# Block sums for the seven-product matmuls: taken one step later, and queued behind the last convolution on VectorE

## The chip, the cores and the metric

The kernel runs on one core of a Trainium2 chip. Its time is the device time of one execution in microseconds (us). Three executions of the kernel before took 2258.66, 2259.78 and 2261.68 us; the median is 2259.78 us. The engines are TensorE (PE; its weight loads are the rows PEld), VectorE (DVE), ScalarE (ACT), GpSimd (POOL) and SyncE (SP). SP and POOL also issue the DMAs that matter here.

## The reference

One inference step of a two-layer streaming encoder, on 1024 prompt frames and 64 sample frames (1088 columns), with 1024 channels. Layer 0 mixes by windowed attention, layer 1 by a diagonal state-space model. Each layer ends in a gated feed-forward net with a causal convolution of width 3; the change touches only this part:

```python
def conv_ffn(h, prev, w_up, conv_w, conv_b, w_down):
    t = h.shape[1]
    up = h @ w_up
    full = jnp.concatenate([prev.astype(up.dtype), up], axis=1)
    c = conv_b
    for j in range(CONV_WIDTH):
        c = c + conv_w[j] * full[:, j:j + t]
    y = (jax.nn.gelu(c[..., :D_FF]) * c[..., D_FF:]) @ w_down
    return y, full[:, -(CONV_WIDTH - 1):]
```

`w_up` is 1024 by 5632, `w_down` 2816 by 1024, `D_FF` is 2816. Everything is float32.

## The kernel before

**Layout.** Channels lie on the 128 partitions, frames along the free axis, in three blocks of 384, 384 and 320 columns. A float32 product is made of three matmuls of rounded parts: each operand is split into a high part (a copy on ACT) and a low part (a subtraction on DVE), and `mm3` (L220) issues L223, L224 and L225. A weight tile is loaded by SP (`raw`), split into `whl` (L193 on ACT and L194 on DVE, or L216 for both), and then used. `unit` (L165) starts the load of a weight tile two tiles ahead of the one that is used.

**The up-projection.** `ffn` runs over 22 gates f. A gate makes two tiles of 128 channels (f and 22 + f): the matmuls give `u`, `conv` (L415) makes `t` from it in one instruction on ACT (L419) and two on DVE (L420, L421; the second is kept as `last_conv`), and the first `t` goes through GELU, is multiplied by the second (L437), and is stored to the DRAM tensor `gd` (L438, L439). In layer 0, and in layer 1 for f under 5, a tile is 3 blocks of 8 by 3 matmuls, evicted by DVE (L411, L413). In layer 1 from f = 5 on, the first two blocks of both tiles are made by `seven` (L491): seven products of half-size blocks in place of eight (Strassen's scheme). DVE takes their results out of PSUM and adds them into `u` at L508, L510, L515, L516, L518, L520 and L521. PSUM holds six such results (`mm_ps`, six buffers); a matmul group can only start when one of the six is free.

**The down-projection** of the first two blocks is made of seven products too (`pair`, L599), in both layers. It needs block sums of the weights and of the gate outputs, which are made beside the up-projection, 11 of each in each layer:

- `sums_w` (L353): a load of 128 by 2048 weights into `jt` (layer 0) or `jw` (layer 1) at L355, four operations on DVE (L358 to L361), a store to `sd` (L362).
- `sums_g` (L365): a load of 128 by 1536 gate outputs from `gd` into `jt` or `jg` (L367), four operations on DVE (L370 to L373), a store to `td` (L374). Number k needs the outputs of the gates k and 11 + k.

The DMAs of these go through SP in layer 0 and through POOL in layer 1 (`Q`, L351), as do the stores of `gd`. There is one `jw` and one `jg`, so a load waits until the store before it has landed; in layer 0 both kinds share one tile `jt`, whose two halves alternate for `sums_g`.

**Steps.** `aside` (L441) is called twice in each gate: between its two convolutions, and after its product. Each call is a step, j = 0 to 43. `sums(j)` (L382) first finishes the jobs that are due at j, then starts the load that `starts` has for j: `sums_w(k)` at the odd steps 2k + 1 (layer 0) or 2k + 13 (layer 1), `sums_g(k)` at the even steps 2k + 24. A job is finished (operations and store) one step after its load, with the load of the last one after the loop:

```python
        def sums(j):

            for x in jobs.pop(j, []):
                next(x, None)
            if j in starts:
                x = starts[j]
                next(x)
                jobs[j + 1] = [x]
```

**What sets the order.** The code says which instruction depends on which; a list scheduler then puts each engine's instructions into one fixed order, from priorities (the order of the code) and from its own estimate of when each is ready. Every engine and every DMA-issuing queue works strictly in that order, so an instruction that waits holds all behind it. `order(x, first)` (L124) makes x stand behind `first` in that order and adds no wait. In layer 0 the preparation of the state-space model (`ssm_prep`; `w`, `kt`, `wps`, `prm`) runs beside the up-projection too.

**After the up-projection**, `pair` runs products 0 to 6, each of 11 steps k by 4 row tiles m by 3 matmuls. `operand(p)` (L565) loads `gr` from `gd` (products 0, 1, 6) or from `td` (products 2 to 5) through SP and splits it into `gt` (L562 on ACT, L563 on DVE). `product` (L587) takes its last three k for two row tiles at a time. The results are taken out of PSUM by ACT for product 0 (L611) and by DVE otherwise (L613).

Of the kernel before, what the change touches and what calls it, by code (L numbers as in the profile page):

```python
# [22 lines left out]
KF = DFF // P  # L23
# [20 lines left out]
class Core:  # L44
# [295 lines left out]
    def ffn(self, i, h, rb, after, side=None, beside=lambda: None, x=None, g=None):  # L340
# [10 lines left out]
        E, Q = nc.vector, (nc.sync, nc.gpsimd)[i]  # L351

        def sums_w(k):  # L353
            x = (jt[:, :2048] if i == 0 else self.yp.tile([P, 2048], F32, name="jw", tag="ypB", bufs=1)).rearrange("p (c h m) -> p c h m", c=2, h=2)
            Q.dma_start(x, a["w_down"][i, k::KH].rearrange("c p (h m) -> p c h m", h=2))  # L355
            yield
            a11, a12, a21, a22 = x[:, 0, 0], x[:, 1, 0], x[:, 0, 1], x[:, 1, 1]
            E.tensor_add(a22, a21, a22)  # L358
            E.tensor_sub(a21, a11, a21)
            E.tensor_sub(a11, a22, a11)  # L360
            E.tensor_sub(a12, a12, a11)  # L361
            Q.dma_start(sd[:, k], x)  # L362

        def sums_g(k):
            x = jt[:, k % 2 * 1536:k % 2 * 1536 + 1536] if i == 0 else ts.tile([P, 1536], F32, name="jg", tag="t2")  # L365
            x = x.rearrange("p (c b t) -> p c b t", c=2, b=2)
            Q.dma_start(x, gd[:, k::KH, :768].rearrange("p c (b t) -> p c b t", b=2))  # L367
            yield
            a11, a12, a21, a22 = x[:, 0, 0], x[:, 0, 1], x[:, 1, 0], x[:, 1, 1]
            E.tensor_sub(a11, a12, a11)  # L370
            E.tensor_sub(a12, a22, a12)
            E.tensor_sub(a22, a22, a11)
            E.tensor_sub(a21, a21, a22)  # L373
            Q.dma_start(td[:, k], x)  # L374


        w0 = (PLAIN + 1) * i
        starts = {2 * (k + w0) + 1: sums_w(k) for k in range(KH)}
        starts.update({2 * (k + KH) + 2: sums_g(k) for k in range(KH)})
        jobs = {}  # L380
# [5 lines that stand above are left out]
            if j in starts:  # L386
                x = starts[j]
                next(x)
                jobs[j + 1] = [x]

        def u_tile(m):
            u = self.t4([P, T + 4], "u")
# [50 lines left out]
        def aside():  # L443

            j = next(turns) + 1
            if side is not None and j <= SIDE:
                with self.later(LOW):
                    next(side, None)
            sums(j - 1)
# [84 lines left out]
        for f in range(1, KF):  # L534
# [14 lines left out]
                us = up([f, KF + f, f + 1])  # L549
            gate(f, us)  # L550
            aside()
        for j in range(2 * KF, 2 * KF + 2):
            sums(j)
        if i == 1:
            ts_ctx.__exit__(None, None, None)
# [1044 lines left out]
```

## Time and profile before

| | us |
|---|---|
| three executions, median | 2259.78 |
| the profiled execution: its time | 2264.88 |
| the profiled execution: its span, first to last instruction | 2263.1 |
| PE busy in the span | 2201.7 |
| DVE busy | 1688.5 |
| ACT busy | 1019.2 |
| POOL busy | 415.2 |
| matmuls of the up-projection of layer 0 | 372 to 934 |
| matmuls of the up-projection of layer 1 | 1503 to 1999 |
| seven products of layer 1 (down-projection), from | 1999 |

A busy row of an engine counts the instructions of that engine in the profile; the time of the profiled execution holds 1.8 us beyond its span. In a row of the timeline the columns are: start and duration in us, engine, line, operation, tile written and tiles read, shapes, count, and in brackets the idle time of that engine just before, with what ended it. A row of the view of waits has the instruction that waited, the instruction that released it, the total in us, the number of times, and the longest.

### The profile page before, as it was taken

How to read it: one execution, taken by the hardware profiler on the slowest of the kernel's cores; microseconds unless marked ns; L12 is line 12 of the kernel's file. 1: busy time of each engine (PE TensorE's matmuls, PEld its weight loads, DVE VectorE, ACT ScalarE, POOL GpSimd, SP SyncE). 2: the span in 40 equal slices, each digit the busy share in tenths (PEclk: the TensorE clock that was granted, in tenths of full speed). 3: DMA queues.
4: the chain of work that ended last, by engine and by line, in shares of the span. 5: the costliest groups of instructions: out<-in, count | busy, mean ns of one | idle time of the engine just before them, and what ended most of it. 6: DMA issues, size and time to landing. Idle time of an engine off the chain costs nothing. (4 is left out here: it accounts for less than half of the span.)

```text
span 2263.1 us, 36074 instructions
## 1 busy us (share of the span) xinstructions
PE 2201.7 (97%) x13875; PEld 2122.4 (94%) x13875; DVE 1688.5 (75%) x2954; ACT 1019.2 (45%) x1839; POOL 415.2 (18%) x474
## 2 busy tenths in 40 slices
PE   8999999999999999999998899999999999999997
PEld 8987789999999999999996799999999999989997
DVE  8677647989877777667767855588997787686764
ACT  5255747422333343455534641263544444355543
POOL 5322004200042423000200034352011011100000
PEclk9999999999999999999998999999999999999999
DMA  5100014656345565887749888652266577578773
GB/s 195 37 21 29 16 65 151 242 191 211 107 138 185 178 203 179 259 288 222 227 164 339 262 286 300 234 166 74 96 233 218 213 287 258 193 250 278 222 256 99
DMA packets 208124, 428.48 MB, mean 189 GB/s; under 512 B 23312, under 2 KB 114224, under 8 KB 205008
## 3 DMA queue, kind: packets, MB, share of 16 engines
q1 hardware_dynamic: 175648, 326.56, 44.0%
q0 software_dynamic: 23984, 95.12, 11.6%
q10 hardware_dynamic: 8320, 4.49, 0.9%
q8 instruction: 109, 1.79, 0.3%
q14 instruction: 63, 0.52, 0.1%
HBM read 297.75 MB, written 128.37 MB: 188 GB/s over the span
## 5 line engine op out<-in xcount | busy, mean ns | idle before, releaser
L223 PE MATMUL mm<-hl,whl 128*128 128x384 f32 (+1 forms) x1960 | 643.8, 329 | 7.7 <-DVE hl L306 3.1
L225 PE MATMUL mm<-hh,whl 128*128 128x384 f32 (+1 forms) x1960 | 641.1, 328 | 2.3 <-DVE whl L216 2.3
L224 PE MATMUL mm<-hh,whl 128*128 128x384 f32 (+1 forms) x1960 | 642.2, 328 | 0.0
L223 PEld LDWEIGHTS mm<-hl,whl 128*128 128x128 f32 x1960 | 368.4, 188 | 10.8 <-DVE hl L306 4.5
L225 PEld LDWEIGHTS mm<-hh,whl 128*128 128x128 f32 x1960 | 368.4, 188 | 2.9 <-DVE whl L216 2.9
L224 PEld LDWEIGHTS mm<-hh,whl 128*128 128x128 f32 x1960 | 368.7, 188 | 0.0
L216 ACT ACTIVATE whl<-raw 128x1024 fp32r<-128x1024 f32 x202 | 212.9, 1058 | 339.1 <-PE mm L225 176.4
L216 DVE TENSOR_TENSOR whl<-raw,whl 128x1024 fp32r<-128x1024 f32 x202 | 254.4, 1263 | 96.7 <-ACT whl L216 96.2
L223 PE MATMUL mm<-gt,whl 128*128 128x384 f32 (+1 forms) x968 | 318.5, 329 | 7.9 <-DVE y L613 3.6
L225 PE MATMUL mm<-gt,whl 128*128 128x384 f32 (+1 forms) x968 | 316.9, 328 | 0.7 <-DVE whl L216 0.7
L224 PE MATMUL mm<-gt,whl 128*128 128x384 f32 (+1 forms) x968 | 317.3, 328 | 0.0
L223 PEld LDWEIGHTS mm<-gt,whl 128*128 128x128 f32 x968 | 182.9, 189 | 10.5 <-DVE y L613 4.9
L225 PEld LDWEIGHTS mm<-gt,whl 128*128 128x128 f32 x968 | 182.7, 189 | 1.0 <-DVE whl L216 1.0
L224 PEld LDWEIGHTS mm<-gt,whl 128*128 128x128 f32 x968 | 182.8, 189 | 0.0
L194 DVE TENSOR_TENSOR whl<-raw,whl 128x1024 fp32r<-128x1024 f32 x84 | 96.3, 1153 | 73.0 <-ACT whl L193 72.4
L193 ACT ACTIVATE whl<-raw 128x1024 fp32r<-128x1024 f32 x84 | 82.6, 986 | 126.8 <-DMA raw<-sd 51.0
L419 ACT ACTIVATE t<-u,ppt 128x1090 f32<-128x1090 f32 x88 | 114.2, 1298 | 50.6 <-DVE u L521 24.6
L420 DVE SCALAR_TENSOR_TENSOR t<-u,ppt,t 128x1090 f32<-128x1090 f32 x88 | 123.6, 1406 | 9.8 <-ACT t L419 9.1
L421 DVE SCALAR_TENSOR_TENSOR t<-u,ppt,t 128x1090 f32<-128x1090 f32 x88 | 123.4, 1403 | 0.4
L563 DVE TENSOR_TENSOR gt<-gr,gt 128x768 fp32r<-128x768 f32 (+2 forms) x106 | 90.2, 880 | 10.7 <-ACT gt L562 10.1
L331 POOL TENSOR_TENSOR y<-y,xl 128x768 f32<-128x768 f32 (+1 forms) x16 | 31.3, 1954 | 354.0 <-DVE y L328 288.0
L562 ACT ACTIVATE gt<-gr 128x768 fp32r<-128x768 f32 (+2 forms) x106 | 78.3, 771 | 39.5 <-DMA gr<-gd 30.2
(390 smaller groups left out, 4181.0 us busy)
## 6 DMA issues: line engine op xcount, KB each, us to landing
raw<-in_w_up SPq DMA_DIRECT2D x88, 512.0 KB, 4.3
raw<-in_w_down SPq DMA_DIRECT2D x74, 512.0 KB, 4.5
raw<-sd SPq DMA_DIRECT2D x40, 512.0 KB, 4.6
sj<-in_w_up POOLq DMA_DIRECT2D x68, 256.0 KB, 6.4
su<-sj POOLq DMA_DIRECT2D x34, 512.0 KB, 5.8
raw<-su SPq DMA_DIRECT2D x34, 512.0 KB, 4.8
pm<-prm SPq DMA_DIRECT2D x32, 522.0 KB, 8.2
gr<-td SPq DMA_DIRECT2D x40, 384.0 KB, 5.9
```

The costliest lines, as they stand in the source:

```text
L193: nc.scalar.activation(w[:, 0], raw, AF.Copy)
L194: nc.vector.tensor_sub(w[:, 1], raw, w[:, 0].bitcast(F32))
L216: x = nc.scalar.activation(w[:, 0], raw, AF.Copy), nc.vector.tensor_sub(w[:, 1], raw, w[:, 0].bitcast(F32))
L223: nc.tensor.matmul(out, w[:, 0, sl], xl, start=start, stop=False)
L224: nc.tensor.matmul(out, w[:, 0, sl], xh, start=False, stop=False)
L225: self.last_mm = nc.tensor.matmul(out, w[:, 1, sl], xh, start=False, stop=stop)
L331: x = by[q].tensor_add(yq, yq, xs[q])
L419: nc.scalar.activation(t, u[:, 0:T + 2], AF.Identity, bias=cb(m), scale=cw(0, m))
L420: nc.vector.scalar_tensor_tensor(t, u[:, 1:T + 3], cw(1, m), t, op0=ALU.mult, op1=ALU.add)
L421: self.last_conv = nc.vector.scalar_tensor_tensor(t, u[:, 2:T + 4], cw(2, m), t, op0=ALU.mult, op1=ALU.add)
L562: nc.scalar.activation(x[:, 0, u], raw, AF.Copy)
L563: nc.vector.tensor_sub(x[:, 1, u], raw, x[:, 0, u].bitcast(F32))
```

## The change

Both kinds of sums are finished two steps after their load instead of one, the loop after the last gate has one step more for it, and the first of the four operations of each is ordered behind the last convolution that the code has issued by then. (Each line after L358 moves down by one, by an empty line.)

```diff
@@ -355,7 +355,8 @@
             Q.dma_start(x, a["w_down"][i, k::KH].rearrange("c p (h m) -> p c h m", h=2))
             yield
             a11, a12, a21, a22 = x[:, 0, 0], x[:, 1, 0], x[:, 0, 1], x[:, 1, 1]
-            E.tensor_add(a22, a21, a22)
+
+            self.order(E.tensor_add(a22, a21, a22), self.last_conv)
             E.tensor_sub(a21, a11, a21)
             E.tensor_sub(a11, a22, a11)
             E.tensor_sub(a12, a12, a11)
@@ -367,7 +368,7 @@
             Q.dma_start(x, gd[:, k::KH, :768].rearrange("p c (b t) -> p c b t", b=2))
             yield
             a11, a12, a21, a22 = x[:, 0, 0], x[:, 0, 1], x[:, 1, 0], x[:, 1, 1]
-            E.tensor_sub(a11, a12, a11)
+            self.order(E.tensor_sub(a11, a12, a11), self.last_conv)
             E.tensor_sub(a12, a22, a12)
             E.tensor_sub(a22, a22, a11)
             E.tensor_sub(a21, a21, a22)
@@ -386,7 +387,7 @@
             if j in starts:
                 x = starts[j]
                 next(x)
-                jobs[j + 1] = [x]
+                jobs[j + 2] = [x]
 
         def u_tile(m):
             u = self.t4([P, T + 4], "u")
@@ -549,7 +550,7 @@
                 us = up([f, KF + f, f + 1])
             gate(f, us)
             aside()
-        for j in range(2 * KF, 2 * KF + 2):
+        for j in range(2 * KF, 2 * KF + 3):
             sums(j)
         if i == 1:
             ts_ctx.__exit__(None, None, None)
```

The order of the instructions differs between the two kernels in the up-projection of layer 0 and its end, and in layer 1 from gate 5 on and its end; between these two places it is the same on every engine.

Where the change moves instructions, first place: DVE in layer 1, gate 19 (its `u` tiles are u_18399 and u_18402 before, u_18394 and u_18397 in the changed kernel). Before:

```order
L515 TENSOR_TENSOR u_18402<-u_18399,mm_18502 128x384
L516 TENSOR_TENSOR u_18399<-u_18399,mm_18457 128x384
L518 TENSOR_TENSOR u_18399<-u_18399,mm_18517 128x384
L370 TENSOR_TENSOR jg_18584<-jg_18584 128x384
L371 TENSOR_TENSOR jg_18584<-jg_18584 128x384
L216 TENSOR_TENSOR whl_18699<-raw_18697,whl_18699 128x1024
L372 TENSOR_TENSOR jg_18584<-jg_18584 128x384
L520 TENSOR_TENSOR u_18402<-u_18402,mm_18536 128x384
L420 SCALAR_TENSOR_TENSOR t_18579<-u_18399,ppt_88,t_18579 128x1090
L373 TENSOR_TENSOR jg_18584<-jg_18584 128x384
L521 TENSOR_TENSOR u_18402<-u_18402,mm_18517 128x384
L421 SCALAR_TENSOR_TENSOR t_18579<-u_18399,ppt_88,t_18579 128x1090
```

The same gate on DVE in the changed kernel:

```order
L516 TENSOR_TENSOR u_18397<-u_18394,mm_18497 128x384
L517 TENSOR_TENSOR u_18394<-u_18394,mm_18452 128x384
L519 TENSOR_TENSOR u_18394<-u_18394,mm_18512 128x384
L216 TENSOR_TENSOR whl_18694<-raw_18692,whl_18694 128x1024
L521 TENSOR_TENSOR u_18397<-u_18397,mm_18531 128x384
L421 SCALAR_TENSOR_TENSOR t_18574<-u_18394,ppt_88,t_18574 128x1090
L522 TENSOR_TENSOR u_18397<-u_18397,mm_18512 128x384
L422 SCALAR_TENSOR_TENSOR t_18574<-u_18394,ppt_88,t_18574 128x1090
L371 TENSOR_TENSOR jg_18384<-jg_18384 128x384
L394 MEMSET u_18594 128x2
L394 MEMSET u_18597 128x2
L372 TENSOR_TENSOR jg_18384<-jg_18384 128x384
```

Before, the first sum of `jg` (L370) stands between two evictions of the same gate (L518 and L520); now all evictions of that gate (the last are L521 and L522) and its first convolution stand ahead of it, and the `jg` that is summed there is the one whose load was issued a gate earlier.

Second place: DVE at the head of the feed-forward net of layer 0, where block 2 of the input is normalized (`hl`, `sqb`, `nvsqb`). Before:

```order
L306 SCALAR_TENSOR_TENSOR hl_3944<-q_507,ppt_88,hh_3943 128x320 x3
L358 TENSOR_TENSOR jt_4581<-jt_4581 128x512
L271 TENSOR_SCALAR nvsqb_3932<-pr_3928 128x3
L272 RECIPROCAL nvsqb_3932<-nvsqb_3932 128x3
L359 TENSOR_TENSOR jt_4581<-jt_4581 128x512
L289 TENSOR_TENSOR nvsqb_3932<-nvsqb_3932 128x3
L331 TENSOR_TENSOR q_507<-q_507,xl_3842 128x640
L256 TENSOR_TENSOR sqb_3967<-sqb_3967,sqb_3969 128x640
L360 TENSOR_TENSOR jt_4581<-jt_4581 128x512
L290 TENSOR_TENSOR nvsqb_3932<-nvsqb_3932 128x3
L306 SCALAR_TENSOR_TENSOR hl_3944<-q_507,ppt_88,hh_3943 128x320 x2
L361 TENSOR_TENSOR jt_4581<-jt_4581 128x512
```

In the changed kernel:

```order
L306 SCALAR_TENSOR_TENSOR hl_3944<-q_507,ppt_88,hh_3943 128x320 x3
L271 TENSOR_SCALAR nvsqb_3932<-pr_3928 128x3
L272 RECIPROCAL nvsqb_3932<-nvsqb_3932 128x3
L289 TENSOR_TENSOR nvsqb_3932<-nvsqb_3932 128x3
L331 TENSOR_TENSOR q_507<-q_507,xl_3842 128x640
L290 TENSOR_TENSOR nvsqb_3932<-nvsqb_3932 128x3
L256 TENSOR_TENSOR sqb_3967<-sqb_3967,sqb_3969 128x640
L291 SCALAR_TENSOR_TENSOR nvsqb_3932<-nvsqb_3932 128x3
L306 SCALAR_TENSOR_TENSOR hl_3944<-q_507,ppt_88,hh_3943 128x320 x2
```

The four operations of the first `jt` are gone from between the two groups of L306; the first of them now stands behind convolutions of the gates 0 and 1.

Third place: the end of the up-projection of layer 1 in POOL's queue (`gd` of gate 20 and 21, and the last `jg`). Before:

```order
L374 DMA td1_14570<-jg_18784 128x1536
L438 DMA gd1_14568<-t_18779 128x1024
L439 DMA gd1_14568<-t_18779 128x64
L367 DMA jg_18984<-gd1_14568 128x2x768
L556 DMA out_o_conv<-cst_14567 128x176
L374 DMA td1_14570<-jg_18984 128x1536
L438 DMA gd1_14568<-t_18979 128x1024
L439 DMA gd1_14568<-t_18979 128x64
L367 DMA jg_18999<-gd1_14568 128x2x768
L374 DMA td1_14570<-jg_18999 128x1536
```

In the changed kernel:

```order
L368 DMA jg_18784<-gd1_14568 128x2x768
L439 DMA gd1_14568<-t_18774 128x1024
L440 DMA gd1_14568<-t_18774 128x64
L557 DMA out_o_conv<-cst_14567 128x176
L375 DMA td1_14570<-jg_18784 128x1536
L439 DMA gd1_14568<-t_18974 128x1024
L440 DMA gd1_14568<-t_18974 128x64
L368 DMA jg_18984<-gd1_14568 128x2x768
L375 DMA td1_14570<-jg_18984 128x1536
L368 DMA jg_18999<-gd1_14568 128x2x768
L375 DMA td1_14570<-jg_18999 128x1536
```

Before, one load of `jg` (number 10) and one store of `td` stand behind the last store of `gd`; now two of each (numbers 9 and 10) stand there, one after the other.

## The prediction, made before the changed kernel was run

> **What bounds the kernel now.** I read the page first, then the waits of PE by stretch, then the timeline around each of them.
>
> ```profile
> PE 2201.7 (97%) x13875; PEld 2122.4 (94%) x13875; DVE 1688.5 (75%) x2954; ACT 1019.2 (45%) x1839; POOL 415.2 (18%) x474
> ```
>
> PE is busy for 97% of the span, so a change on DVE can only win what PE waits for DVE; all of PE's idle time is 2263.1 - 2201.7 = 61 us, and most of it lies in stages that the change does not reach. PE's waits (who waited, for whom: us in total, times, longest) in layer 0's feed-forward net (370 to 1010 us), in layer 1's up-projection (1660 to 2050), and behind it (2050 to 2120):
>
> ```profile
> PE wps L1073 <- DVE kt L1067: 4.4, 3, 1.7
> PE mm L223 <- DVE hl L306: 3.1, 3, 1.6
> PE wps L1073 <- DVE w L887: 2.9, 3, 1.2
> ...
> PE mm L223 <- DVE u L520: 4.9, 3, 2.1
> PE mm L223 <- ACT y L611: 0.9, 1, 0.9
> ...
> PE mm L223 <- DVE y L613: 2.8, 2, 1.8
> ```
>
> About 19 us of waits are within reach, and only a part of them has to do with the sums. What DVE itself waits for, from the view of the tiles jg, jt and jw:
>
> ```profile
>   DMA jg<-gd: 31.3, 7
>   DMA jt<-gd: 18.3, 4
>   DMA jt<-in_w_down: 11.3, 7
>   DMA jw<-in_w_down: 7.9, 4
> ```
>
> That is 31.3 + 18.3 + 11.3 + 7.9 = 69 us of DVE standing in front of a load that has not landed. The reader should not take this for the gain: of seven stalls on jg only three reach PE. Here are those three, and one that does not (DVE first, then PE, where it waited):
>
> ```profile
> 1933.82 0.56 DVE L370 TENSOR_TENSOR jg<-jg 128x384 f32<-128x384 f32 x1 [6.61 <-DMA jg<-gd]
> ...
> 1956.40 0.56 DVE L370 TENSOR_TENSOR jg<-jg 128x384 f32<-128x384 f32 x1 [6.08 <-DMA jg<-gd]
> 1959.08 0.55 DVE L520 TENSOR_TENSOR u<-u,mm 128x384 f32<-128x384 f32 x1
> 1959.68 0.44 PE L223 MATMUL mm<-hl,whl 128*128 128x384 f32 x1 [1.06 <-DVE u L520]
> ...
> 1980.13 0.56 DVE L370 TENSOR_TENSOR jg<-jg 128x384 f32<-128x384 f32 x1 [7.24 <-DMA jg<-gd]
> 1982.80 0.55 DVE L520 TENSOR_TENSOR u<-u,mm 128x384 f32<-128x384 f32 x1
> 1983.40 0.44 PE L223 MATMUL mm<-hl,whl 128*128 128x384 f32 x1 [1.72 <-DVE u L520]
> ...
> 2002.88 1.23 DVE L194 TENSOR_TENSOR whl<-raw,whl 128x1024 fp32r<-128x1024 f32 x1 [2.79 <-ACT whl L193]
> 2004.89 0.56 DVE L370 TENSOR_TENSOR jg<-jg 128x384 f32<-128x384 f32 x1 [0.78 <-DMA jg<-gd]
> 2005.36 0.55 DVE L520 TENSOR_TENSOR u<-u,mm 128x384 f32<-128x384 f32 x1
> 2005.97 0.44 PE L223 MATMUL mm<-gt,whl 128*128 128x384 f32 x1 [2.14 <-DVE u L520]
> ```
>
> The sum stands ahead of the eviction L520 in DVE's order, its load is late, the eviction is late with it, and the next group of matmuls finds no free PSUM buffer. The three waits are 1.06 + 1.72 + 2.14 = 4.92 us, all that the row L520 holds.
>
> **The change part by part.** No operation is added or removed: 44 sums with four operations each, 88 DMAs. Only their places move.
>
> *Layer 1, the gates.* The sums of jg now stand behind all evictions of their gate, so none of the three rows above has a sum between PE and its eviction. The load is issued a gate earlier than its sum. A gate takes 23 us (from 1933.82 over 1956.40 to 1980.13, above), and a transfer of this tile:
>
> ```profile
> DMA to landing us min/median/max: 3.5/6.4/8.2
> ```
>
> Before such a load POOL waits for the store of td, which for number 5 took from 1903.72 to 1910.70:
>
> ```profile
> 1903.72 0.53 POOL L374 DMA_DIRECT2D td<-jg  x1 [7.69 <-DVE u L516]
> 1910.70 0.72 POOL L367 DMA_DIRECT2D jg<-gd  x1 [6.44 <-DMA td<-jg]
> ```
>
> So 7 + 8.2 = 15 us at most lie between a sum and its successor's data, against 23: the load has landed. In the last gate the wait of 2.79 us for a weight split (row 2002.88) would remain if that row stayed ahead of the eviction; in the new order it stands behind both. I take all **4.9 us**; bounds 2.8 (if the third wait stays) and 4.9. What is late next on PE there: nothing in the window but the 0.9 us of L611. What is queued behind the moved sums on DVE is the second convolution, the product L437 and the store of gd; they come later by four operations of 0.56 us at most, and gd of a gate is read a gate later at the earliest. On POOL, gd now stands behind a store of td that is ready half a gate earlier, so it is not held.
>
> *Layer 0, head.* The first jt is summed amid the normalization of block 2, for which PE waits:
>
> ```profile
> 404.82 0.68 DVE L358 TENSOR_TENSOR jt<-jt 128x512 f32<-128x512 f32 x1
> ...
> 409.43 1.00 DVE L306 SCALAR_TENSOR_TENSOR hl<-q,ppt,hh 128x320 fp32r<-128x320 f32 x2
> ...
> 410.02 0.41 PE L223 MATMUL mm<-hl,whl 128*128 128x320 f32 x1 [1.58 <-DVE hl L306]
> ...
> 408.00 2.06 POOL L303 TENSOR_SCALAR gx<-q,ppt 128x320 f32<-128x320 f32 x1
> 410.13 1.03 POOL L304 TENSOR_TENSOR hl<-gx,hh 128x320 fp32r<-128x320 f32 x1
> ...
> 370.00:700.00 330.00, 324.73 (x1997) 322.81 (x1996) 288.28 (x651) 117.88 (x182) 55.89 (x38) 1.00 0.54 180
> ```
>
> Three operations of 0.68 us (L358 and, like it, L359 and L360) leave the way to L306: 2 us, more than the 1.58. But the last of the eight rows of hl comes from POOL at 410.13 + 1.03 = 411.16. The last row, a stretch with its busy times (PE first), gives 330 / 1997 = 0.165 us for a matmul, so 0.5 us for the three of one hl. Without its wait PE starts at 410.02 - 1.58 = 408.44 and wants POOL's hl three of these later, at 409.9: there it waits for up to 1.26 us instead. The gain lies between 1.58 - 1.26 = 0.3 and 1.58; I take **0.7**, nearer to the end that POOL's row sets, since POOL ran into that row without a gap.
>
> [...]
>
> *Layer 0, the rest.* The stalls on jt (18.3 + 11.3 us) reach PE nowhere: its other waits there are for w and kt of the state-space preparation, 4.4 + 2.9 = 7.3 us, and the new order keeps these at the same places between the convolutions. DVE is less often stalled, but 11 sums of 4 times 0.69 us move into the stretch from 570 to 700 us, where they did not stand. I take 0; bounds -3 (each of the six waits longer by half a microsecond) and +7.3. On SP the load of the next jt now stands right behind the store of the last. Weights are loaded two tiles ahead, and the distance of that store and load was at least this:
>
> ```profile
> 411.75 0.34 SPq L362 DMA_DIRECT2D sd<-jt  x1
> 415.56 0.37 SPq L355 DMA_DIRECT2D jt<-in_w_down  x1
> ```
>
> So a weight load may come some 4 us later; a tile of weights lasts 72 matmuls of 0.165 us, 12 us, and two tiles 24 us. That hides it, unless the hold were six times as long.
>
> *Layer 1, the end.* Before, one load of jg hung behind the last store of gd:
>
> ```profile
> 2019.15 0.55 POOL L438 DMA_DIRECT2D gd<-t  x1 [6.07 <-DVE t L437]
> 2026.02 0.72 POOL L367 DMA_DIRECT2D jg<-gd  x1 [5.79 <-DMA gd<-t]
> 2036.60 0.56 POOL L374 DMA_DIRECT2D td<-jg  x1 [9.86 <-DVE jg L373]
> ...
> raw<-sd SPq DMA_DIRECT2D x40, 512.0 KB, 4.6
> ...
> gr<-td SPq DMA_DIRECT2D x40, 384.0 KB, 5.9
> ```
>
> Now two hang there, in series. Number 8's td leaves at about 2017 and lands 7 us later; load 9 at 2024, landed at 2031 (6.4 us), summed by 2034 (four operations), stored by 2041, load 10 landed at 2048, summed by 2051, landed in DRAM at 2058: 15 us later than before (2036.60 + 7 = 2043). Product 2 begins at the row 2054.47 below and takes the td of number 10 last: its first use is the 37th of 44 triples, 36 / 44 of the 25.1 us between the two rows, so at 2075. A load of gr of 5.9 us (the last row: median from issue to landing) and its split, 2 us by two rows of the kind of L194, end at 2066: 9 us early. The other user of DVE's time there is the eviction L613, at the ends of products 1 and 2:
>
> ```profile
> 2054.47 0.44 PE L223 MATMUL mm<-gt,whl 128*128 128x384 f32 x1 [1.02 <-DVE y L613]
> ...
> 2079.58 0.45 PE L223 MATMUL mm<-gt,whl 128*128 128x384 f32 x1 [1.77 <-DVE y L613]
> ```
>
> The sums of number 10 stand just ahead of the first of these in the new order, and are done by 2051 plus 1.2 us for one weight split: L613 at 2052.2 to 2053.2, where it now runs at 2053.87. So it is a near thing, and I take 0 for these two waits, with bounds of -3 (loads 9 and 10 at 8.2 us and not 6.4, their stores a microsecond slower) and +2.8. The wait of 0.93 us at the end of product 0 comes from a split on ACT that waits for gr from td between two evictions L611; in the new order that split stands behind all four. I take **+0.9**.
>
> **Sum.** 4.9 + 0.7 + 0.9 = 6.5 us off the profiled execution: 2264.88 - 6.5 = 2258.4 us. That execution was 5.1 us above the median of the runs shown, so against the median the forecast is 2259.78 - 6.5 = **2253.3 us**, 0.29% faster. A measurement of this kernel can tell about 0.2% (4.5 us) from no change.
>
> **The rivals.**
>
> *PE hides it (2258 us).* For: of seven stalls on jg four cost PE nothing, and PE may have been paced by something just behind, so that a removed wait comes back some matmuls later (weights, or POOL's hl at the head). Against: each gate runs without any wait where no stall falls on L520, and in 1660 to 2050 there is no other wait than these 5.8 us. If half of 4.9 comes back and the two small terms are nothing, 2.5 us are left: 2259.8 - 2.5 = 2257.3; with a loss of 1 at the end 2258. Chance 0.26.
>
> [...]
>
> *The serial end holds product 2 and 3 (2266 us).* The two loads in series end later than 2058. SP works in order, and in its new order the loads of the operand of product 3 and the first weights of product 3 stand behind the gr of number 10. Those weights are needed at 2079, and a weight load with its split takes some 7 us (4.6 and 2): from a landing at 2072 on, 14 us later than I have it, each microsecond stops PE for one. If each of the five transfers in series (7, 6.4, 7, 6.4, 7 us) took twice as long, the landing would be 34 us late and PE would stand for 20 us; for a result slower than before by 0.2% it takes 11 us, a landing at 2083. With 12 to 13 us it is 2266. Against: the longest transfer of that tile was 8.2 us. Chance 0.06.
>
> *DVE gets ahead everywhere (2248 us).* The w and kt waits (7.3) or the ones of L613 (2.8) go in part as well: 5 us more. Chance 0.08.
>
> **How the numbers follow.** Forecast 0.60, PE hides it 0.26, the serial end 0.06, ahead everywhere 0.08. The forecast's own terms run from 2.8 + 0.2 - 1 to 4.9 + 1.6 + 3, so from 2 to 9.5 us: it lies under the line of 2255.3 us (0.2%) with about nine parts in ten of its chance. Faster: 0.54 + 0.08 + 0.02 of the first rival's = 0.64. Slower 0.06. The same: 0.30. The range takes in the first rival and most of the third: 2249 to 2260.
>
> **What would show it.** Right: no wait of DVE for jg, jt or jw inside the gates; no wait of PE for L521 (the new number of that eviction); PE busy 389 of 390 us in that stretch; a smaller wait of PE for hl at 410 us. Wrong: PE waiting for another eviction in the same gates, for wps longer than 7.3 us in all, or for L614 (the old L613) at the ends of products 1 and 2 for more than 2.8 us; a td of number 10 that leaves after 2060; a gr of product 2 as the releaser of a matmul.

## The result, and the profile after

The change makes the kernel slower. Twenty executions of the changed kernel have a median of 2265.02 us (2257.06 to 2277.05), twenty of the kernel before beside them 2258.63 us (2254.57 to 2261.68): a ratio of 1.0028, interval 1.0018 to 1.0039, so 6.4 us more where 6.5 us less were forecast. The executions of the changed kernel also spread over 20 us, those of before over 7. The profiled execution of the changed kernel is the slowest of its twenty; I read in it where time goes, and take sizes from the medians.

In the changed kernel each line after L358 is one higher than before (L520 is L521, L887 is L888); all other kernels here keep the numbers of before. The busy times of its page, PE first:

```profile
PE 2206.9 (97%) x13875; PEld 2126.2 (93%) x13875; DVE 1696.1 (75%) x2954; ACT 1016.6 (45%) x1839; POOL 418.7 (18%) x474
```

What DVE waits for, by the tiles jg, jt and jw of the changed kernel (us, times):

```profile
  DMA jg<-gd: 1.5, 2
...
  DMA jt<-gd: 0.6, 1
  DMA jt<-in_w_down: 0.2, 1
...
  DMA jw<-in_w_down: 1.2, 1
```

DVE stood 69 us in front of these loads before and stands 3.5 us now. The change does what its words say, and the kernel is slower. The waits of PE in the changed kernel, for layer 0's up-projection (370 to 1010 us):

```profile
PE wps L1074 <- DVE w L888: 9.1, 5, 3.6
PE wps L1074 <- DVE kt L1068: 2.3, 2, 1.4
PE mm L223 <- DVE gt L564: 1.7, 1, 1.7
PE mm L223 <- DVE hl L306: 1.5, 2, 0.9
```

and for layer 1 from 1660 to 2050 us (the first row) and from 2050 to 2120 (the second):

```profile
PE mm L223 <- ACT y L612: 2.8, 2, 2.3
...
PE mm L223 <- DVE y L614: 2.3, 2, 1.9
```

In layer 1 the 4.9 us on the eviction (L520, now L521) are gone. In layer 0 the wait for hl fell from 3.1 to 1.5 us as the sum left its way, but the waits for w and kt grew from 7.3 to 11.4 us and one for gt came up. A second loss stands behind the long waits. Windows of the changed kernel (the fields with (x) are busy times, PE first; the third last number is the granted clock of TensorE):

```profile
660.16:663.57 3.41, 1.27 (x10) 1.15 (x11) 3.41 (x8) 0.00 (x0) 1.24 (x1) 1.00 0.41 163
663.57:666.98 3.41, 3.41 (x14) 3.41 (x13) 3.41 (x6) 2.05 (x5) 3.33 (x3) 0.50 0.63 245
779.62:783.04 3.42, 1.44 (x10) 1.44 (x11) 3.42 (x6) 2.03 (x4) 1.41 (x2) 1.00 0.00 0
783.04:789.86 6.82, 6.00 (x22) 5.52 (x21) 6.43 (x10) 3.10 (x6) 4.55 (x4) 0.50 0.59 189
```

After the wait of 3.6 us at 662 us and the one of 2.8 us at 782 us the clock is 0.50 for 3.4 and 6.8 us. What that costs shows in the matmuls behind the first of them (timeline of PE in the changed kernel):

```profile
662.30 0.66 PE L1074 MATMUL wps<-ident,w 128*128 128x128 f32 x4 [3.63 <-DVE w L888]
...
662.98 0.34 PE L223 MATMUL mm<-hl,whl 128*128 128x384 f32 x1
663.15 0.34 PE L224 MATMUL mm<-hh,whl 128*128 128x384 f32 x1
...
664.30 0.52 PE L223 MATMUL mm<-hl,whl 128*128 128x384 f32 x1
664.62 0.52 PE L224 MATMUL mm<-hh,whl 128*128 128x384 f32 x1
```

A matmul starts every 0.32 us instead of 0.17, so nearly half of those 10.2 us is lost, by estimate 4 to 5 us. In the profiled execution of before the clock is 1.00 through this whole net (370 to 1010 us). With 4.2 us of longer waits (14.6 in the rows above against 10.4) that is 8 to 9 us; PE's first down-projection matmul of layer 0 starts at 942.94 us, 8.45 us later than before (934.49). The two profiled executions differ by 12.2 us in all. About 4 us of that arise between 1010 and 1500 us, where the order of the instructions is the same in both kernels, so no moved instruction explains them.

One caution on these waits: the kernels l1_only and l1_only_b below have layer 0 in the order of before, and in their profiles the waits for w and kt are 3.5 and 2.4 us, not 7.3. So a single profile gives the size of such a wait only roughly.

### The profile page after: what moved, and what is told of

It reads as the page before. It is cut to its first block, busy times and chain, and to the rows that moved or that the text cites. A ratio compares the mean times of both kernels' runs of the same rounds, so it can differ in the third digit from the quotient of the medians.

```text
span 2275.3 us, 36086 instructions
## 1 busy us (share of the span) xinstructions
PE 2206.9 (97%) x13875; PEld 2126.2 (93%) x13875; DVE 1696.1 (75%) x2954; ACT 1016.6 (45%) x1839; POOL 418.7 (18%) x474
## 4 chain that ended last, share of the span: by engine, by line
PE 28%; DMA 13%; DVE 9%; issue 4%; ACT 3%; POOL 1%; SPq 0%; ACTq 0%; DVEq 0%; POOLq 0%
PE mm L223 8%; PE mm L225 8%; PE mm L224 8%; DMA raw<-in_w_down 4%; DMA sj<-in_w_up 2%; DVE whl L216 1%; DMA raw<-sd 1%; DMA yd<-ys 1%; DVE whl L194 1%; DMA raw<-in_w_up 1%; ACT whl L216 1%; DVE y L328 1%; ACT whl L193 1%; PE pb L223 1%; PE pb L225 1%
## 5 line engine op out<-in xcount | busy, mean ns | idle before, releaser
L412 DVE TENSOR_TENSOR u<-rb,mm 128x384 f32<-128x384 f32 (+1 forms) x164 | 80.6, 503 | 40.7 <-PE mm L225 35.8
```

What stands on the lines that cost most here:

```text
L412: nc.vector.tensor_mul(u[:, t0 + 2:t0 + 2 + np_], rb[:, t0:t0 + np_], ps[:, :np_])
```

## The experiments

All runs were timed beside the kernel before; the ratio of the two decides, since the median of before moves between 2251 and 2254 us from one set of these runs to the next. A median is one of 5 to 12 executions.

| run | what differs from before | median us | ratio | interval |
|---|---|---|---|---|
| l1_only | the change, layer 1 alone | 2249.15 | 0.998 | 0.9969 to 0.9992 |
| l1_only_b | the same again | 2241.52 | 0.9962 | 0.9948 to 0.9977 |
| l1_head | l1_only, and layer 0's first sum of weights | 2245.21 | 0.9974 | 0.9959 to 0.9988 |
| l1_head_b | the same again | 2242.01 | 0.9965 | 0.9952 to 0.9977 |
| l0_only | the change, layer 0 alone | 2265.51 | 1.0053 | 1.0036 to 1.007 |
| l0_order | layer 0, order without the step | 2261.24 | 1.0031 | 1.0015 to 1.0046 |
| l0_step | layer 0, step without the order | 2253.43 | 0.9996 | 0.9985 to 1.0006 |
| l0_w | layer 0, sums of weights alone | 2258.49 | 1.0029 | 1.0014 to 1.0043 |
| l0_w_small | l0_w with short operations | 2258.62 | 1.0022 | 1.001 to 1.0035 |
| l0_g | layer 0, sums of gate outputs alone | 2262.64 | 1.0047 | 1.0028 to 1.0066 |
| l0_g_q | l0_g, stores of td through POOL | 2262.56 | 1.0042 | 1.0028 to 1.0056 |
| l0_g_late | l0_g, two stores of td moved back | 2255.43 | 1.002 | 1.0009 to 1.003 |
| l0_g_late2 | l0_g_late, one weight load moved forward | 2255.88 | 1.0001 | 0.999 to 1.0012 |
| best_d | l1_head, stores of td through POOL | 2253.31 | 1.0003 | 0.999 to 1.0016 |
| all_fix | the whole change, layer 0's transfers moved | 2251.46 | 0.9999 | 0.9988 to 1.001 |
| all_fix2 | all_fix, one weight load moved forward | 2249.11 | 0.9986 | 0.9975 to 0.9997 |
| l0_fill, l0_fill2 | l0_only with spare matmuls | 2274.38, 2268.96 | 1.0105, 1.0072 | 1.0083 to 1.0127, 1.005 to 1.0094 |

### Which layer, and which half of the change

The edit of l1_only; in l0_only it is `i == 0` and `2 - i`; l0_order has the order alone and l0_step the step alone:

```diff
+        behind = lambda v: self.order(v, self.last_conv) if i == 1 else v
-            E.tensor_add(a22, a21, a22)
+            behind(E.tensor_add(a22, a21, a22))
-            E.tensor_sub(a11, a12, a11)
+            behind(E.tensor_sub(a11, a12, a11))
-                jobs[j + 1] = [x]
+                jobs[j + 1 + i] = [x]
-        for j in range(2 * KF, 2 * KF + 2):
+        for j in range(2 * KF, 2 * KF + 3):
```

> The change in layer 1 alone, layer 0 as before. Theory A (layer 0 loses, layer 1 wins): the three waits of PE for the eviction L520 are gone (4.9 us), the waits for w and kt in layer 0 stay at about 7 us in all with no half-clock stretch there, and the time is 2 to 5 us under the kernel before. Theory B (the end of layer 1 gives it back: in the trace of the whole change the waits for L611 and L613 at the ends of the first products rose from 3.8 to 5.1 us and two stretches of 3.4 us there ran at half clock instead of one): within 1.5 us of before. Theory C (layer 1 costs as much as layer 0): 3 us or more above before.

> The change in layer 0 alone, layer 1 as before. Theory A: the waits of PE for w and kt (L887, L1067) are 10 to 12 us in all instead of 7.2, one or more of them over 2 us, with half-clock stretches of 3.4 us behind these; the wait for hl at 410 us is gone and is not seen at 662 us any more; time 7 to 11 us above before, with a spread of 10 us or more between runs. Theory B: about 6 us above. Theory C (both layers share the loss): 3 us above.

> Layer 0 with the sums behind the last convolution, but still one step after their load; layer 1 as before. If the place in DVE's queue between the convolutions and w and kt is what costs (four operations of 0.69 us ahead of w or kt at each of the six waits): waits for w and kt of 9 us or more, time 4 to 9 us above before. If the load's place in SP's queue is what costs (the load of jt right behind the store, ahead of the store of prm): within 2 us of before.

> Layer 0 with the sums two steps after their load, but not ordered behind the convolution; layer 1 as before. DVE's order hardly differs from before, SP's differs at a few loads and stores of jt. If DVE's queue is what costs: within 2 us of before. If the place of jt's load and store on SP costs: 4 to 9 us above.

Layer 1 alone is 0.2% faster (0.4% in the repeat, below), layer 0 alone 0.5% slower: theory A. (One detail of it missed: in l1_only the waits for w and kt were 3.5 us, not about 7.) In layer 0 the step alone does nothing, the order alone costs 0.3%.

By their expectations these last two speak for DVE's queue and against SP's. They do not settle it, because a store follows its sums: the order on DVE alone moves transfers on SP too. In l0_order a store of td stands among the eight loads of `tl` in the third step of the preparation (at 712.60 us, between loads that begin at 709.83 and 713.19).

### Which of the sums of layer 0

l0_w and l0_g take the edit of l0_only for one kind of sum:

> Layer 0, the sums of the weights alone in the new manner (behind the convolution, two steps after their load); the sums of the gate outputs and layer 1 as before. On DVE eight sum operations stand between ct and kt of the first preparation step and three in the second, where before none did; on SP the loads of tl are not split. Theory A (two places cost: the sums of the weights at 660 us through DVE's queue, the sums of the gates at 780 and 860 us through SP's queue): a wait for w of 3 to 4 us at 662 us with a half-clock stretch behind it, the later waits for w and kt under 0.7 us each as in the run of layer 1 alone; time 4 to 7 us above before. Rival (the loss needs both kinds of sums): within 2 us of before.

> Layer 0, the sums of the gate outputs alone in the new manner; the sums of the weights and layer 1 as before. DVE has no sum operation ahead of w or kt that was not there before; on SP the store of td stands in the middle of the eight loads of tl at the fifth and seventh preparation step, not behind them. Theory A: no long wait at 662 us (under 2 us), waits for w and kt at 780 and 860 us up by 1 to 2 us each against the run of layer 1 alone; time 2 to 6 us above before. Rival (only DVE's queue counts): within 1.5 us of before.

Both kinds cost: l0_w within its expected range, l0_g more than expected. In l0_w the wait at 662 us was 1.8 us, not 3 to 4, and the long one (2.8 us, with the half clock behind it) stood at 700 us. In l0_g the waits at 780 and 860 us rose to 2.9 and 3.0 us, as expected of SP's order, and the loss was 0.47%.

### DVE's queue or SP's queue

Two runs were to tell the two queues apart. In l0_w_small the operations take `[:, :64]` of their operands, so this kernel leaves out seven eighths of layer 0's sums of the weights; in l0_g_q the store reads `nc.gpsimd.dma_start(td[:, k], x)`.

> As the run with the sums of the weights alone in layer 0 (l0_w), but layer 0's four operations of each sum of weights take 64 of the 512 columns, so each lasts some 0.2 us instead of 0.69; loads and stores stay whole, near their places. It leaves out seven eighths of layer 0's sums of the weights. Theory D (the four operations between ct and w lengthen DVE's chain by 2.4 us at 660 and at 700 us): the waits at 660 and 700 us fall from 1.8 and 2.8 us to about 1 us each, no half-clock stretch at 700 us, and the time is 3 us or more under l0_w. Rival (SP's order, with the load of jt ahead of the store of prm): as l0_w within 1.5 us.

> As the run with the sums of the gate outputs alone in layer 0 (l0_g), with one change: in layer 0 the store of td goes through POOL's queue and not through SP's; PE's order is the same and DVE's nearly. Theory S (in l0_g the store of td stands between the fourth and the fifth of the eight loads of tl in SP's order, holds the rest and lands ahead of them, so that tp, ct and w are late): the waits for w and kt at 780 and 860 us fall from 2.9 and 3.0 us to under 1.5 us each, tp no longer waits over 4 us for tl there, and the time is 4 us or more under that of l0_g, so 1 to 6 us above before. Rival (DVE's queue, or the transfers themselves, whichever queue issues them): waits and time as in l0_g, within 2 us.

Neither theory D nor theory S held for the time, which came out as the rivals had it, or nearly. With short operations the loss hardly fell (1.0022 against 1.0029). But these intervals are wide, so DVE's part in l0_w stays open: the wait at 700 us did fall from 2.8 to 0.7 us, as theory D had it, while the wait at 660 us rose from 1.8 to 2.3 us. With the store of td off SP's queue the loss stayed (1.0042 against 1.0047). A third run made the same edit in a kernel that has no loss:

> As the kernel with the change in layer 1 and the first sum of weights of layer 0 (l1_head), with layer 0's stores of td through POOL's queue; the order on PE, DVE and ACT is the same, and SP no longer has a store of td behind the loads of tl, ahead of a weight load and the store of prm. Theory S+: the waits for w and kt from 740 us on fall by 1 to 3 us in all, the time is 1 to 3 us under l1_head, 9 to 11 us under before. Rival (the store on SP costs nothing where it stands behind the loads): as l1_head within 1 us, some 7 us under before.

The order on PE, DVE and ACT is that of l1_head, and the kernel lost what l1_head had gained (1.0003 against 0.9974). Timelines of l1_head and of best_d, the sixth step of the preparation:

```profile
826.26 6.20 SPq L1094 DMA_DIRECT2D tl<-kd  x8
832.56 0.53 SPq L374 DMA_DIRECT2D td<-jt  x1
...
834.32 2.00 ACT L1095 ACTIVATE tp<-tl 128x1024 f32<-128x1024 f32 x1 [2.39 <-DMA tl<-kd]
```

```profile
828.77 6.91 SPq L1094 DMA_DIRECT2D tl<-kd  x8
831.10 0.55 POOL L374 DMA_DIRECT2D td<-jt  x1 [3.41 <-DVE jt L373]
837.70 2.00 ACT L1095 ACTIVATE tp<-tl 128x1024 f32<-128x1024 f32 x1 [3.79 <-issue]
```

On SP the store stood behind the eight loads of tl; through POOL it starts in the middle of them. tp then starts 837.70 - 828.77 = 8.9 us after the first load, not 834.32 - 826.26 = 8.1, and PE's waits for w and kt from 740 to 910 us rise from 3.5 to 5.4 us. Both expectations missed. In l0_g_q it is the same, in the step at 750 us: there the store starts from POOL 1.97 us after the first load of tl (749.77 against 747.80), and tp starts 11.29 us after that load (759.09). (The profile puts the end of ACT's wait down to a weight load there.) So in these runs the step came later where a store started among its loads, also when POOL issued it.

The 0.3% of best_d need not be all due to that, however. SP's order differs from l1_head's in one more place, a load of `xl` and a weight load at the end of the net. SP in l1_head, and then in best_d:

```profile
914.65 0.37 SPq L191 DMA_DIRECT2D raw<-in_w_down  x1
921.74 0.87 SPq L317 DMA_DIRECT2D xl<-x  x2
```

```profile
925.99 0.36 SPq L317 DMA_DIRECT2D xl<-x  x1
926.40 0.46 SPq L191 DMA_DIRECT2D raw<-in_w_down  x1
```

Behind it PE waits 1.6 us (for gt and y, from 900 to 1050 us) where l1_head has no wait. What this place costs is measured next; in best_d the two causes were not separated. l0_g and l0_g_q both have the load of xl in front, so their comparison is free of it.

### Moving the transfers alone

In l0_g two of the stores of td stand in the middle of the loads of tl on SP. l0_g_late puts them behind the last load and leaves PE, DVE and ACT as they are:

```diff
-            Q.dma_start(td[:, k], x)
+            v, n = Q.dma_start(td[:, k], x), {1: 3, 4: 5}.get(k); i == 0 and n in self.tls and self.order(v, self.tls[n])
-            nc.sync.dma_start(dst, src)
+            self.tls = {**getattr(self, "tls", {}), q: nc.sync.dma_start(dst, src)}
```

> As the run with the sums of the gate outputs alone in layer 0 (l0_g, 9.7 us above before), with two stores of td, which stood between the fourth and the fifth load of tl, behind the eighth. The order on PE, DVE and ACT is the same. Theory T (a transfer of the sums that starts ahead of the loads of tl delays them, whichever queue issues it): tp comes 17.4 to 18 us after kt in the fourth and sixth preparation step, not 19.8; the waits for w and kt at 780 and 860 us fall from 2.9 and 3.0 us to under 1.5 us each; time 5 us or more under l0_g, within 4 us of before. Rival (DVE's queue, or the loads' own later start): tp, waits and time as in l0_g, within 2 us.

SP and ACT in l0_g, and then in l0_g_late:

```profile
749.54 2.52 SPq L1094 DMA_DIRECT2D tl<-kd  x4
752.15 0.55 SPq L374 DMA_DIRECT2D td<-jt  x1
752.75 3.32 SPq L1094 DMA_DIRECT2D tl<-kd  x4
...
758.53 2.01 ACT L1095 ACTIVATE tp<-tl 128x1024 f32<-128x1024 f32 x1 [4.19 <-DMA tl<-kd]
```

```profile
747.41 5.17 SPq L1094 DMA_DIRECT2D tl<-kd  x8
752.67 0.53 SPq L374 DMA_DIRECT2D td<-jt  x1
...
755.39 2.00 ACT L1095 ACTIVATE tp<-tl 128x1024 f32<-128x1024 f32 x1 [2.60 <-DMA tl<-kd]
```

From the first load to tp: 8.99 us with the store among the loads, 7.98 behind them. The waits for w and kt from 740 to 870 us fall from 5.9 us to 2.4, and the ratio from 1.0047 to 1.002: more than half of the loss, by two stores. The rival of this run is out.

What was left showed at the end of the net (PE waited 1.3 us for gt at 931 us and 2.1 us for y at 1030). SP's order differs there in one more place: a load of xl (L317) had come to stand ahead of a weight load (L191) of the down-projection. The scheduler had put it there; the change does not touch either. l0_g_late2 orders the loads of xl behind that weight load (the fifth at L191), nothing else:

> As l0_g_late (4.1 us above before), with one weight load of SP (the fifth of the down-projection of layer 0) back ahead of the two loads of xl, where it stood before the change; the order on PE, DVE and ACT is the same. Theory X (the load of xl waits until 920 us for its buffer and holds the weight load 8 us, whose split then holds the splits of gt and their users): the weight load is issued at some 913 us, PE's wait for gt at 931 us (1.35 us) and the ones for y at 1030 us (2.1 us) go, and the time is 2 to 4 us under l0_g_late, within 2 us of before. Rival (the later store of td holds the end): waits and time as in l0_g_late.

SP and ACT in l0_g_late, and then in l0_g_late2:

```profile
920.22 0.36 SPq L317 DMA_DIRECT2D xl<-x  x1
920.63 0.46 SPq L191 DMA_DIRECT2D raw<-in_w_down  x1
...
926.70 1.06 ACT L193 ACTIVATE whl<-raw 128x1024 fp32r<-128x1024 f32 x1 [6.75 <-DMA raw<-in_w_down]
```

```profile
916.78 0.37 SPq L191 DMA_DIRECT2D raw<-in_w_down  x1
922.83 0.87 SPq L317 DMA_DIRECT2D xl<-x  x2
...
923.77 1.06 ACT L193 ACTIVATE whl<-raw 128x1024 fp32r<-128x1024 f32 x1 [1.53 <-DMA raw<-in_w_down]
```

The load of xl waits for a free buffer, until the preparation's last store of tp (prm<-tp) has landed, and SP waits with it: 6.7 us in the changed kernel (`SPq L317 <- DMA prm<-tp: 6.7, 1, 6.7`), and in l0_g_late it starts 7.9 us after that store does (920.22 against 912.29); the weights behind it come late, and with them the splits on ACT and DVE. With the weight load in front PE has no wait from 900 to 1050 us, and the ratio is 1.0001. The loss of l0_g is accounted for by three transfers. The changed kernel has the load of xl in front too:

```profile
930.68 0.87 SPq L317 DMA_DIRECT2D xl<-x  x2
931.59 0.98 SPq L191 DMA_DIRECT2D raw<-in_w_down  x2
```

The same for the whole change, with the loads of jt and the stores of sd between 620 and 700 us moved too:

> The whole change in both layers, with layer 0's transfers of the sums kept out of the way of the preparation: the two stores of td and the stores of sd behind the loads of tl, and the loads of jt behind the store of prm from oc, from 620 to 870 us. The sums stand behind the convolutions and two steps after their loads as in the change. Theory T: the loss of layer 0 is gone but for what DVE's queue takes (0 to 3 us), and the gain of layer 1 is left: 3 to 8 us under before, 9 us or more under the changed kernel. Rival (DVE's place costs on its own): 3 us or more above before, as the changed kernel.

> As all_fix (as before the change, to 0.1%), with the same weight load back ahead of the two loads of xl. Theory X: PE's wait for gt at 936 us (2.1 us) and the half-clock stretch behind it go, time 3 to 6 us under before. Rival: as all_fix within 1.5 us.

Among the transfers of the weights' sums one delay stood here: the load of jt ahead of the store of tp, on which ACT's next step waits. SP and ACT in the changed kernel, and the row that answers in the kernel before:

```profile
639.84 0.38 SPq L355 DMA_DIRECT2D jt<-in_w_down  x1
642.99 0.38 SPq L1097 DMA_DIRECT2D prm<-tp  x1
...
649.53 2.08 ACT L1043 ACTIVATE oc<-ct 128x512 f32<-128x512 f32 x2 [5.57 <-DMA prm<-tp]
```

```profile
646.71 2.14 ACT L1042 ACTIVATE oc<-ct 128x512 f32<-128x512 f32 x2 [0.56 <-DMA prm<-tp]
```

The store of tp (prm<-tp) starts at 642.99 us in the changed kernel and at 642.97 in the kernel before, so SP did not hold it; with the load of jt on its way, the copy to oc, which waits for it, starts 6.5 us after it and not 3.7.

The whole change went from 1.0028 to 0.9999 and 0.9986, every sum still behind its convolution and two steps after its load. all_fix missed its expected 3 us. In all_fix2 the wait for gt is gone as expected; the gain of 0.13% between the two is within their intervals. all_fix2 still lies behind layer 1 alone; its one long wait in the net:

```profile
PE wps L1073 <- DVE kt L1067: 4.8, 3, 3.6
```

There (662 us) three operations of a sum stand ahead of kt on DVE (L358 at 657.28 us, L359 and L360 at 660.54 and 661.25; kt at 661.86). What part of the rest is DVE's was not separated. Nor was a run made that moves only the transfers of the weights' sums, so for these the cause is argued from all_fix and the rows above, not shown by itself.

### The head

> The change in layer 1 alone once more, beside l1_head_b: 4 to 6 us under before, as the first time.

> The change in layer 1 and the first sum of weights of layer 0 once more, beside l1_only_b. If the gain at the head is kept: 1 to 3 us under l1_only_b. If it is given back at 660 us: within 1 us of it.

Side by side the two have one ratio (0.9962 and 0.9965). In l1_head_b the wait for hl at 410 us (1.6 us in l1_only_b) is gone, and PE's wait for kt at 661 us is 1.7 us instead of 1.3. A part of the head's gain is returned there; what is left in this pair is too small to measure.

### Two that failed

Spare matmuls were to keep PE busy in the wait at 662 us and so to keep its clock.

> As the change in layer 0 alone, with 16 spare matmuls (the operands of the last matmul once more, into the bank that the transposes overwrite) in PE's queue where it waits for w at 662 us: some 2.8 us of work inside a wait of 3.9 us, so nothing comes later by itself. Theory H (a long wait also costs clock: the stretch of 6.8 us at half clock behind it): the granted clock stays at 1.00 between 655 and 700 us, PE gets from the transposes at 659 to 663 us to those at 700 us 3 us sooner, and the time is 2 to 3.5 us under the run of layer 0 alone. Rival (the clock drop has another cause, or costs nothing): clock and time as in that run, within 1 us.

> As the change in layer 0 alone, with 12 spare matmuls (2.1 us; the operands of the last matmul once more) ahead of the transposes at 662 us, into the second bank, which waits for nothing; the first attempt wrote into the bank that kt is read from and so waited for kt itself. Theory H (a long wait also costs clock): no half-clock stretch between 655 and 670 us, the wait there 2 us shorter and the transposes no later, PE 1.7 to 3.4 us earlier at 700 us than with the half clock, and the time 1.5 to 3.5 us under that of layer 0 alone. Rival (the clock drop costs nothing that is not waited for later): the later waits for w and kt grow by as much, time within 1 us of that run.

Neither tested it. In l0_fill the matmuls wrote into the bank of which kt had not yet been read, waited 2.9 us for kt, and ran behind the wait; in l0_fill2 the scheduler put them among the matmuls ahead of the wait. Both only added work. That the half clock costs time is read from the matmuls' spacing, above; no run took it away.

## Why the prediction was wrong, step by step

- **Layer 1, the gates (4.9 us): right.** No wait for the eviction is left in the changed kernel or in l1_only_b, and in l1_only only 0.3 us of waits for y in that whole stretch. The two runs of layer 1 alone are 0.2 and 0.38% faster: 4.5 and 8.6 us. That the size fits is in part luck. It came from one profile; in the twelve profiles here of kernels with layer 1 as before these waits add up to 0.3 us (l0_g_q) to 5.6 us (l0_g_late2).
- **Layer 1, the end (0.9 us): the named split moved, and another stood in the way.** In the changed kernel the split that reads td stands behind all four evictions L612, as forecast. But a weight split on ACT stood ahead of the first of them, its load was late, and the wait rose to 2.8 us; in l1_only it was 0.3, in l1_only_b nothing. Nor is this wait a mark of the change: with layer 1 as before it was nothing in l0_g and 3.4 us in l0_w. The rival of the serial end did not come. One sign of it did, the td of number 10 left at 2064.1 us, but no matmul waited for what hangs on it.
- **Layer 0, head (0.7 us): the wait went, and no gain was measured.** All of the 1.58 us vanished. The two POOL rows of the prediction (2.06 and 1.03 us, the last one done at 411.16) are these in the changed kernel, done at 409.28:

```profile
406.69 1.61 POOL L303 TENSOR_SCALAR gx<-q,ppt 128x320 f32<-128x320 f32 x1
408.38 0.90 POOL L304 TENSOR_TENSOR hl<-gx,hh 128x320 fp32r<-128x320 f32 x1
```

  The pair of rows just ahead of them is shorter too: L303 and L304 take 1.21 and 0.88 us (at 404.42 and 405.71 in the changed kernel) where they took 1.72 and 1.44 (404.65 and 406.45 before). So with the sums gone from this stretch POOL's rows were shorter, and the prediction had taken them as fixed; why they were is not shown. But PE then reaches the next fixed point, w and kt, sooner and waits there. That the gain had to pass the six waits for w and kt was not asked.
- **Layer 0, the rest (0, bounds -3 and +7.3): the failed step.** l0_only is 0.5% slower, some 12 us. The text said that the new order "keeps these at the same places between the convolutions", and of SP only that "a weight load may come some 4 us later", which two weight tiles hide. The first is not so: in l0_only three operations of a sum stand among those that make w and kt (from 658.06 to 663.42 us), where none stood before. And both look at the wrong cargo. Behind the moved transfers on SP stood the eight loads of tl and the stores of prm: the preparation's chain, from kt over tl, tp, oc and w to the next transposes. Six waits of PE for its ends, 7.3 us, already stood in the profile, so the chain had no slack there. Moving transfers alone took the loss of l0_g away and brought the whole change from 1.0028 to 0.9986; how much of the loss by the weights' sums is DVE's place stays open. The chain could have been read in the profile of before, as the largest row of DVE's waits from 370 to 1010 us:

```profile
DVE ct L1036 <- ACT tp L1095: 29.9, 7, 6.2
DVE jt L370 <- DMA jt<-gd: 18.3, 4, 5.5
```

  I took the second row for the subject and did not ask what the first one was.
- **The bound of half a microsecond for each of six waits** was too narrow for two reasons: with a store among the loads of tl, tp came a microsecond or more later (8.99 us after the first load in l0_g, 7.98 in l0_g_late), and after the waits of 3.6 and 2.8 us in the changed kernel 3.4 and 6.8 us ran at half clock. No term for the clock stood in the sum. And the range did not even hold this bound: it was added up without layer 0's -3, and with -1 for the -3 of layer 1's end. With both the terms reach a kernel some 3 us slower than before, still short of the 6.4 measured.
- **The end of layer 0 was not in the sum at all**, although the end of layer 1 was worked out: one weight load behind a load of xl, 0.2% by l0_g_late and l0_g_late2; the changed kernel has it so too.

## What to carry to other kernels

When a step is moved, list what stands behind each of its transfers on its queue, and which loads start beside it from any queue, and look up whether anything there already ends in a wait: such a chain has no slack, and a delay of it comes out in that wait (here PE's waits for w and kt, 7.3 us before and 11.4 in the changed kernel). An engine's stalls can be removed almost wholly (from 69 us to 3.5 here) and the kernel be slower. Of a change that acts in several places, run each place alone: layer 1's part, 0.2 to 0.4% faster than before, was worth keeping, and beats both kernels.

## What the runs showed of the hardware

- **Behind some waits the granted clock was 0.50, for 3.41 us or twice that.** In the profiles of the kernel before and of the changed kernel the granted clock is 1.00 or 0.50. Each has one stretch at 0.50 that runs into the end; the 17 others last 3.41 us (ten of them) or 6.83 (seven), and within a profile their starts lie whole multiples of 3.413 us apart (in the kernel before the first at 11.44 us and the next at 1168.56, 339 times that later). I counted PE's idle time in pieces of that length, laid on these starts, between 370 and 2235 us and without the state-space stage (1130 to 1330 us). Five pieces at full clock had 1.77 us or more of it (1.77 in the kernel before; 1.86, 1.98, 2.14 and 2.61 in the changed one), and behind each the clock was 0.50; of the 16 with 1.0 to 1.72 us one was followed by 0.50 (1.30 us, the piece from 1124.37 in the changed kernel). So a wait of 2.14 us that fell on two pieces (up to 2005.97 us in the kernel before; 1.00 and 1.14 us) cost no clock, and one of 1.77 us inside a piece (up to 2079.58) was followed by 3.41 us at 0.50. The wider spread of the changed kernel's times may come from waits of this size; that is my estimate, and no run here shows it.
- **Where a store started among the loads of tl, tp came later, from SP and from POOL alike.** In the step at 750 us tp starts 7.98 us after the first load of tl with the store of td behind the loads (l0_g_late), 8.99 us with it among them on SP (l0_g), and 11.29 us with it among them from POOL (l0_g_q). Two such stores moved back took 0.27% off the time (l0_g_late against l0_g).
